# A decoder layer on one Trainium2 core: the output projection as seven products, its weights prepared in the first up projection

## The chip, the cores and the metric

The kernel runs on one core of one Trainium2 chip. The metric is the time of one execution on the device, in microseconds (us); the time before is the median of three executions. One more execution was recorded by the profiler, and every duration quoted below is from it.

PE is the matrix engine (PEld its weight loads), DVE the vector engine, ACT the scalar engine, POOL the general one, SP the engine that issues nearly all DMAs here. Engines run their own instructions in order and wait for each other through semaphores.

## What is computed

One decoder layer on 1024 tokens of width 1024, all in float32:

```python
x = x + 0.5 * swiglu(rmsnorm(x, g1), w_gu1, w_down1)          # first SwiGLU, inner width 2816
z = rmsnorm(x, g_mix) @ w_in                                  # inputs of three branches and their gates
merged = sum(sigmoid(gate_i) * (y_i @ w_branch_i) for i in "abc")
x = x + merged @ w_out                                        # output projection, 1024 x 1024
x = x + 0.5 * swiglu(rmsnorm(x, g2), w_gu2, w_down2)          # second SwiGLU
```

Branch a is a spatial gating unit, b a latent attention over the tokens, c an attention over 256 memory tokens.

## The kernel before, in words

**Layout.** Activations are held with features on the 128 partitions and tokens along the free dimension, in two halves of 512 tokens. `norm.x(half, c)` is feature tile c (of 8) of one half; a tile of 128 x 2 x 512 holds two of them.

**One product.** A float32 value is split into a high part (ACT copy into a rounded type, L139 or L146) and a low part (DVE subtraction, L142 or L147). `mm3` (L158 to L160) multiplies two split operands by three matmuls, high by high, high by low, low by high, of 128 x 128 weights with 128 x 512 tokens.

**Seven products.** The up projections of both SwiGLUs, the gates and the down projections use a scheme of the Strassen-Winograd kind: weights are four blocks A11, A12, A22, A21 (output tile by half of the input features), the activations four blocks b11, b12, b22, b21 (half of the input features by token half), and seven products of sums of blocks take the place of eight. `sum_steps` forms the weight sums s1 to s4 on DVE (L1443), `weights_later` splits them, `unit_steps` runs a unit: 7 products of 4 x 3 matmuls, giving two output tiles for both token halves. A unit's weight pairs are "a" (A11, A12), "s" (s2, s1), "t" (s3, s4) and "l" (A22); each pair takes one buffer of the tag `whi` and one of `wlo`, 5 of each. `up` runs 18 such units (4 to 21) in the first SwiGLU, with PE's order as written and the other engines' orders set by the planner, which lays the program out on a modelled timeline, in program order among what is ready.

**Jobs in the first up projection.** `weight_jobs` splits weights that are needed later (memory attention, latent attention, spatial gating) and writes high and low parts to DRAM. A job (`rounded`) has two steps: issue the load; then split and issue two stores. `up` runs the steps that are due in a unit through `self.extra`, behind the split of "t". There are 14 jobs, and each unit holds about one first and one second step.

**The stage of the change.** Behind the attention, `branch_pairs` multiplies branch b by its weights, gates it (DVE), adds the sum of the other branches (POOL, L574) and splits the result into `merged`. `project` then runs for each token half and output tile c: load w_out's tiles and split them, 8 x 3 matmuls into one PSUM bank, add to x (DVE, L1155), square for the norm (ACT, L1302; summed on DVE, L1307), store every second tile to x2d. Eight output tiles of two halves are 384 matmuls. While half 1 runs, `norm.first()` gives the norm of half 0 four tasks, one behind each of the first four tiles: column sums and root, the scale turned into rows (`norm_scale`, L425), and `part(0)`, `part(1)`, which multiply by gain and scale (L1344), subtract (L1367) and split b22 and t3.

**The second SwiGLU's start.** `units` takes units 0 and 1 together, with the orders of PE, DVE and ACT as written. It begins with s3 t3 and s4 b22 of both units, which need half 0 alone; after `count`=2 and the next of these 16 groups of three matmuls stands the column sum of half 1 (L394), after `turn`=5 its scale (L425), and then half 1's own norm, b11, b21, t2, t1, t4 follow, each made on DVE and ACT just ahead of the product that takes it.

Of the kernel before, what the change touches and what calls it, by code (L numbers as in the profile page):

```python
# [16 lines left out]
P = 128  # L17
# [32 lines left out]
class Kernel:  # L50
# [350 lines left out]
    def turned_sums(self, acc, parts=1, late=False):  # L401


        nc, n = self.nc, acc.shape[-1] // P
        out = self.stat("ts", NT * 2)[:, :n * parts]
        for t0 in range(0, n, 4):
            m = min(4, n - t0)
            b = self.bank()
# [307 lines left out]
    def weight_jobs(self):  # L716

        self.wkv = self.dram.tile([2, 4, 2, P, D], F32, name="wkv")
        jobs = [self.rounded(self.a["mem_w_kv"][g][:, 2 * c:2 * c + 2], self.wkv[g, c])
                for g in range(2) for c in range(4)]  # L720
        self.wqs = self.dram.tile([3, 2, P, H * QK], F32, name="wqs")
        self.wks = self.dram.tile([2, 2, P, D], F32, name="wks")
        self.wss = self.dram.tile([2, P, D], F32, name="wss")

        def causal(x):
            x = x.rearrange("p (g t) -> p g t", g=SGG)
            self.nc.gpsimd.affine_select(
                out=x, in_=x, compare_op=ALU.is_ge, fill=0.0, base=0,
                pattern=[[0, SGG], [1, P]], channel_multiplier=-1,
            )  # L730
# [4 lines left out]
        when = {}  # L735
        for first, some in ((0, jobs), (1, small)):
            for n, job in enumerate(some):
                for f in range(2):
                    at = when.setdefault(first + 2 * n + f, [])
                    at.insert(0 if f else len(at), lambda job=job: next(job))  # L740
        return when
# [358 lines left out]
    def mixer(self, lat):  # L1100
# [36 lines left out]
        merged = [self.hrows() for _ in range(2)]  # L1137
        for _ in self.branch_pairs(
                1, yb, mc, None, each, lambda d, f, x: self.split(*merged[f][d], x)):
            pass  # L1140
        return merged

    def project(self, merged, norm, sink):

        nc, a = self.nc, self.a
        tasks = []
        for half in range(2):
            for c in range(DT):
                w = self.load(a["w_out"][c])
                b = self.bank()  # L1150
                for k in range(DT):
                    self.mm3(b, w[k], merged[half][k], k == 0, k == DT - 1)
                x, parts = norm.x(half, c), 2 if (half, c) == (1, DT - 1) else 1
                for n in self.parts(parts):
                    nc.vector.tensor_tensor(x[:, n], x[:, n], b[:, n], op=ALU.add)  # L1155
                norm.feed(half, c, parts)
                sink(half, c)
                if tasks:
                    tasks.pop(0)()
            tasks = norm.first() if half == 0 else tasks  # L1160
        for t in tasks:
            t()

    def store(self, rows, half, c):

        cols = slice(half * 512, half * 512 + 512)
        n = 1 if half == 1 and c >= DT - 2 else 2
        if n == 1 or c % 2:
            self.nc.sync.dma_start(
                self.out[c - n + 1:c + 1, :, cols].rearrange("c p t -> p c t"),  # L1170
                rows.t[half, c // 2][:, c % 2 - n + 1:c % 2 + 1])


    def run(self):
# [66 lines left out]
        with self.banks("mixps") as self.pm:  # L1241
            merged = self.mixer(latents)
        with tc.tile_pool(name="f2", bufs=1) as fp, self.banks("f2ps") as self.pm:
            rows = Rows(self)
            for half in range(2):
                for p in range(DT // 2):
                    nc.sync.dma_start(rows.take(half, p), x1d[half, p])
            norm = OpNorm(self, rows, lambda: self.g_ffn2)
            ffn = SwiGLU(self, a["ffn2_w_gu"], a["ffn2_w_down"], fp, norm, 2)
            for f in range(2):  # L1250
                ffn.fetch(f, [ffn.w4] * 4)
            self.project(merged, norm, lambda half, c: keep(x2d, norm.t, half, c))
            E = mybir.EngineType
            with tc.manual_schedule(engines={E.PE, E.DVE, E.Activation}):
                ffn.units(
                    (0, 1), (), ([(0, "a")], [(1, "a")]),
                    [lambda: None, lambda: ffn.fetch(2, [self.x4] * 2)],
                    turn=5, third=(2, None, [lambda: ffn.spill(0, ffn.w4, nc.vector)]), count=2)
# [22 lines left out]
class OpNorm:  # L1281
# [7 lines left out]
    def __init__(self, k, rows, gain, scaled=False):  # L1289
        self.k, self.x, self.t, self.gain, self.scaled = k, rows, rows, gain, scaled  # L1290
        self.acc, self.r, self.s, self.op, self.rows = {}, {}, {}, {}, {}
        self.more = []
# [24 lines left out]
    def tokens(self, half):  # L1317
        k = self.k
        more, self.more = self.more, []
        if half == 0 and not self.scaled:  # L1320
            self.s[half] = k.turned_sums(self.acc.pop(half), late=True)
# [10 lines left out]
    def turn(self, half):  # L1332
        k = self.k
        self.s[half] = k.norm_scale(self.r[half], late=k.last is not None)
# [30 lines left out]
    def low(self, p):  # L1365
        b12 = self.norm(0, p)
        self.k.nc.vector.tensor_tensor(b12, self.rows[p][0], b12, op=ALU.subtract)  # L1367
# [11 lines left out]
    def t2(self, p):  # L1379

        t = self.t.t[1, p]
        self.k.nc.vector.tensor_tensor(t, self.t.t[0, p], t, op=ALU.add)
        return t

    def t1(self, p):

        t = self.t.t[0, 2 + p]
        self.k.nc.vector.tensor_tensor(t, t, self.t.t[1, p], op=ALU.subtract)
        return t

    def t4(self, p):

        t = self.t.t[1, 2 + p]
        self.k.nc.vector.tensor_tensor(t, t, self.t.t[1, p], op=ALU.subtract)
# [3 lines left out]
class Seven:  # L1398
# [11 lines left out]
    def __init__(self, k, w, pool, norm):  # L1410
        self.k, self.nc, self.norm, self.w, self.pool = k, k.nc, norm, w, pool
        self.quad, self.made, self.mark, self.extra = {}, {}, None, []
# [20 lines left out]
    def sum_steps(self, f, rooms=None, order="3241"):  # L1433
# [5 lines left out]
        of = {"3": (s3, a11, a21, ALU.subtract), "2": (s2, a22, s3, ALU.subtract),  # L1439
              "4": (s4, a12, s2, ALU.subtract), "1": (s1, a21, a22, ALU.add)}  # L1440
# [13 lines left out]
    def weights_later(self, f, part, room=None):  # L1454
        k, q = self.k, self.quad[f]
# [21 lines left out]
    def unit_steps(self, f, after=False):  # L1477
# [32 lines left out]
        w |= self.weights(f, "l")  # L1510
        del self.quad[f]
# [134 lines left out]
class Gates(Seven):  # L1646
# [49 lines left out]
    def run(self):  # L1696
# [10 lines left out]
        with k.tc.manual_schedule(engines={E.PE}):  # L1707
            for n, f in enumerate(units):
# [4 lines left out]
                self.extra += self.later[:1] + [lambda x=x: got.append(next(x)) for x in jobs.get(n, ())]  # L1713
# [173 lines left out]
class SwiGLU(Seven):  # L1887
# [22 lines left out]
    def emit(self, f, i, half, row, ps, into=None):  # L1910
# [10 lines left out]
        elif half == 0:  # L1921
            self.add(h, row, ps)
        else:
            self.add(row, row, ps)
            self.gate(f, 0, row)
# [150 lines left out]
    def up(self, first, jobs={}):  # L2076

        with self.k.tc.manual_schedule(engines={mybir.EngineType.PE}):
            for f in range(first, FT):
                if f not in self.quad:  # L2080
                    self.fetch(f)
                self.extra += jobs.get(f - first, [])
# [178 lines left out]
def layout(inputs):  # L2261
# [47 lines left out]
    r["w_out"] = cols(i["w_out"].reshape(D, D), P)  # L2309
# [22 lines left out]
```

## Time and profile before

| | |
|---|---|
| median of 3 executions | 2163.2 us (2163.03 to 2163.79) |
| the profiled execution | 2163.03 us, span from first to last instruction 2161.3 us |
| granted PE clock, mean | 0.999 of full speed |
| DMA | 342.56 MB, mean 158 GB/s, nearly all through SP's queue |
| first up projection | 98.2 to 440.9 us |
| attention's end, last branch, output projection | about 1384 to 1527 us |
| first two units of the second SwiGLU | from 1527 us |

A row of a timeline reads: start, duration, engine, line, operation, output<-input by the program's names, shape, count, and in brackets the idle time ahead of it with what ended it. A row of a window reads: from and to, length, then busy time with instructions of PE, PEld, DVE, ACT and POOL, the granted clock, the busy share of the 16 DMA engines and the GB/s they moved. A row of the DMA view gives size and the median time from issue to landing. A "busy" PE is not PE at its peak, because overlapping matmuls have modelled ends; starts are recorded.

### The profile page before, as it was taken

The page shows a single profiled execution, that of the slowest core. Times are in us where ns is not written, and L with a number is a line of the kernel's source. Part 1 is how long each engine was busy: PE and PEld are TensorE (multiplying, and loading weights), DVE is VectorE, ACT ScalarE, POOL GpSimd, SP SyncE. Part 2 cuts the span into 40 slices and gives each one's busy share as a digit, 9 for nine tenths or more (in the row PEclk, how much of TensorE's full clock was granted, in tenths as well). Part 3 has the DMA queues.
Part 4 walks back from the last instruction along what each step waited for, and adds up shares of the span by engine and source line. Part 5 has one row for each costly group of instructions (what it writes and reads, how often), then busy time and mean ns, then how long its engine had stood idle before and what let it go on. Part 6 is the DMA issues. An engine that isn't in the chain of part 4 may idle for free.

```text
span 2161.3 us, 27448 instructions
## 1 busy us (share of the span) xinstructions
PE 2151.9 (100%) x10112; PEld 1797.8 (83%) x10112; DVE 1572.1 (73%) x2371; ACT 910.3 (42%) x1486; POOL 255.0 (12%) x256
## 2 busy tenths in 40 slices
PE   9999999999999999999999999999999999999999
PEld 6888888888887888888988889988888888888887
DVE  7966666679889657655786679886876666657884
ACT  6433333243455434433555378833433223224332
POOL 0011111100000000000123311240011212110000
PEclk9999999999999999999999999999999999999999
DMA  4264555385332445641587832293133332347443
GB/s 148 92 220 159 190 180 175 119 318 193 118 124 94 147 164 180 223 149 61 212 283 259 314 105 69 75 348 104 40 127 103 110 97 100 103 144 288 169 129 104
DMA packets 137175, 342.56 MB, mean 158 GB/s; under 512 B 21713, under 2 KB 30033, under 8 KB 137041
## 3 DMA queue, kind: packets, MB, share of 16 engines
q1 hardware_dynamic: 136896, 340.81, 45.9%
q8 instruction: 79, 1.29, 0.2%
q14 instruction: 56, 0.45, 0.1%
q10 hardware_dynamic: 144, 0.00, 0.0%
HBM read 230.90 MB, written 109.86 MB: 158 GB/s over the span
## 4 chain that ended last, share of the span: by engine, by line
PE 91%; DVE 6%; ACT 1%; DMA 1%; issue 1%; SPq 0%; POOL 0%; ACTq 0%; DVEq 0%; POOLq 0%
PE one L158 15%; PE one L159 15%; PE one L160 15%; PE bank L158 13%; PE bank L159 13%; PE bank L160 13%; PE mm L158 1%; PE mm L159 1%; PE mm L160 1%; PE bank L1019 1%; PE one L1967 1%; DVE w L147 1%; DVE wlo L147 1%; DVE pr L997 1%; DVE wlo L142 1%
## 5 line engine op out<-in xcount | busy, mean ns | idle before, releaser
L146 ACT CAST whi<-x 128x1024 fp32r<-128x1024 f32 x202 | 192.3, 955 | 414.4 <-DVE x L1443 170.4
L147 DVE TENSOR_TENSOR wlo<-x,whi 128x1024 fp32r<-128x1024 f32 x202 | 241.2, 1195 | 58.9 <-ACT whi L146 19.6
L1471 DVE TENSOR_TENSOR t<-t,one 128x512 f32<-128x512 f32 x188 | 128.9, 686 | 190.8 <-PE one L160 190.7
L158 PE MATMUL bank<-h,whi 128*128 128x512 f32 x636 | 247.9, 390 | 0.0
L160 PE MATMUL bank<-h,wlo 128*128 128x512 f32 x636 | 247.5, 389 | 0.0
L159 PE MATMUL bank<-h,whi 128*128 128x512 f32 x636 | 247.5, 389 | 0.0
L158 PE MATMUL one<-h,whi 128*128 128x512 f32 x508 | 199.0, 392 | 0.0
L159 PE MATMUL one<-h,whi 128*128 128x512 f32 x508 | 198.4, 390 | 0.0
L160 PE MATMUL one<-h,wlo 128*128 128x512 f32 x508 | 198.3, 390 | 0.0
L158 PE MATMUL one<-w,whi 128*128 128x512 f32 x432 | 168.5, 390 | 0.0
L159 PE MATMUL one<-w,whi 128*128 128x512 f32 x432 | 168.1, 389 | 0.0
L160 PE MATMUL one<-w,wlo 128*128 128x512 f32 x432 | 168.1, 389 | 0.0
L142 DVE TENSOR_TENSOR wlo<-w,whi 128x1024 fp32r<-128x1024 f32 (+2 forms) x112 | 114.4, 1036 | 67.3 <-ACT whi L139 67.1
L139 ACT CAST whi<-w 128x1024 fp32r<-128x1024 f32 (+2 forms) x112 | 98.8, 901 | 149.8 <-PE one L159 55.6
L2067 POOL TENSOR_TENSOR raw<-raw 128x512 f32<-128x512 f32 x38 | 57.0, 1499 | 794.8 <-DVE raw L1908 684.8
L160 PEld LDWEIGHTS bank<-h,wlo 128*128 128x128 f32 x636 | 119.4, 188 | 24.9
L159 PEld LDWEIGHTS bank<-h,whi 128*128 128x128 f32 x636 | 119.4, 188 | 24.6
L158 PEld LDWEIGHTS bank<-h,whi 128*128 128x128 f32 x636 | 119.4, 188 | 24.4
L158 PE MATMUL bank<-whi 128*128 128x512 f32 x352 | 136.9, 389 | 0.0
L159 PE MATMUL bank<-wlo,whi 128*128 128x512 f32 x352 | 136.9, 389 | 0.0
L160 PE MATMUL bank<-whi,wlo 128*128 128x512 f32 x352 | 136.9, 389 | 0.0
L160 PEld LDWEIGHTS one<-h,wlo 128*128 128x128 f32 x508 | 95.8, 189 | 20.1
(406 smaller groups left out, 4892.2 us busy)
## 6 DMA issues: line engine op xcount, KB each, us to landing
x<-in_ffn_w_gu_dram SPq DMA_DIRECT2D x78, 512.0 KB, 5.1
w<-tdt SPq DMA_DIRECT2D x40, 512.0 KB, 4.2
gate<-raw SPq DMA_DIRECT2D x33, 512.0 KB, 3.0
tdb<-raw SPq DMA_DIRECT2D x64, 256.0 KB, 2.1
h<-in_ffn_w_down_dram SPq DMA_DIRECT2D x64, 256.0 KB, 6.0
w<-tdb SPq DMA_DIRECT2D x30, 512.0 KB, 5.1
tdt<-w SPq DMA_DIRECT2D x48, 256.0 KB, 2.4
x<-in_w_gate_dram SPq DMA_DIRECT2D x22, 512.0 KB, 5.9
```

The costliest lines, as they stand in the source:

```text
L139: i = self.nc.scalar.copy(hi, src)
L142: return (eng or self.nc.vector).tensor_tensor(lo, src, hi.bitcast(F32), op=ALU.subtract)
L146: self.nc.scalar.copy(hi, src)
L147: return lambda: self.nc.vector.tensor_tensor(lo, src, hi.bitcast(F32), op=ALU.subtract)
L158: i = mmul(out, s[0], m[0], start=first, stop=False, **kw)
L159: mmul(out, s[0], m[1], start=False, stop=False, **kw)
L160: self.last = mmul(out, s[1], m[0], start=False, stop=last, **kw)
L997: nc.vector.tensor_tensor_reduce(out=pr[:, :m], in0=sc[:, :m], in1=self.mask[:, m0:m0 + m], scale=1.0, scalar=-NEG, op0=ALU.add, op1=ALU.m ...
L1019: nc.tensor.transpose(b[:, at:at + P], prs[t][:, kk * P:(kk + 1) * P], self.ident)
L1471: return self.nc.vector.tensor_tensor(out, x, y, op=ALU.add)
L1967: k.last = nc.tensor.matmul(b, w, norm.x(half, c), start=c == 0, stop=c == DT - 1)
L2067: sub = lambda d, x, y: (eng or nc.gpsimd).tensor_tensor(d, x, y, op=ALU.subtract)
```

## The change

The output projection becomes seven products too, four output tiles deep, and runs in a new function `merge` together with branch b. `project` and the call of `branch_pairs` for branch b are gone. w_out is laid out by the host as blocks A11, A12, A22, A21, each in two groups g of 128 x 1024.

```diff
+        for u, b in product("a", self.single, ws, "b11", True):      # product 1, A11 b11, banks kept
+            add(1, 2 * u + 1, b, ALU.subtract)
...
+        for u, b in product("x", self.bank, w2, "t2", True):         # 2
...
+        for u, b in product("x", None, ws, "t1", False):             # 3, on top of 2
...
+        for u, b in product("x", None, w2, "b22", False):            # 4, on top
+            add(0, 2 * u, b)
+            norm.feed(0, 2 * u)
...
+        for u, b in product("y", self.bank, ws, "t3", True):         # 5
+            add(0, 2 * u + 1, b)
+            norm.feed(0, 2 * u + 1)
+            sink(0, 2 * u + 1)
+        ws = weights(6)
+        later()
+        norm.take = self.single
+        for u, b in product("a", None, w2, "b21", False):            # 6, on top of 1
+            add(1, 2 * u, b)
+            if u == 1:
+                with self.tc.high_priority(offset=600):
+                    norm.sums(0)
+            elif u == 3:
+                norm.turn(0)
+                norm.take = None
+                norm.part(0)
+            norm.feed(1, 2 * u)
+        for u, b in product("y", None, ws, "t4", False):             # 7, on top of 5
+            parts = 2 if u == 3 else 1
+            if u == 0:
+                norm.part(1)
+            add(1, 2 * u + 1, b, parts=parts)
+            norm.feed(1, 2 * u + 1, parts)
+            sink(1, 2 * u + 1)
```

(The comments are added here.) `product` runs u = 0 to 3, each 4 blocks x 3 matmuls, into four banks. Ahead of it, `merge` runs branch b in 16 steps ordered by block (b11, b12, b22, b21), with gating and addition both on DVE, and splits b11, t2, b22, t1, t3, b21, t4. `weights(n)` only loads split parts from DRAM, four loads of 512 KB a product. `manual_schedule` keeps the order of PE and SP as written throughout `merge`; the loads of x from DRAM (`load`) stand behind `weights(1)`. The two token halves change places (x1d, x2d and `store` are indexed the other way), and signs in the seven products are turned (`plus`), with the same number of operations.

The weights are made in the first up projection. Their sums are formed in DRAM by DMAs that POOL issues, plain copies and adding ones, one step in each of units 0 to 10 of `up`:

```diff
+        def move(d, x, more):
+            self.nc.gpsimd.dma_start(d, x, max_dma_last_dim=2 * D, **({"accum_op": ALU.add} if more else {}))
...
+        steps = ((s3, A11, False), (s1, A21, False), (s3, A21, True), (s1, A22, True),
+                 (s2, s3, False), (s2, A22, True), (s4, s2, False), (s4, A12, True))
+        return [lambda x=x: blocks(*x) for x in steps] + [first, second, third]
```

The eight `steps` are two DMAs of 512 KB each, for w_out; `first` (4 x 512 KB), `second` (6 x 256 KB) and `third` (4 x 256 KB) form the sums of units 0 and 1 of the second SwiGLU. Then 20 more jobs (`rounded`) split them: 14 for the seven weights of the output projection in two groups, 6 for "a", "t" and "s" of the second SwiGLU's units 0 and 1. Jobs have two places in a unit now: the old one behind "t" (`ahead`), and one behind the split of "l" (`behind`):

```diff
+        made = [self.rounded(x.unsqueeze(1), d) for x, d in parts]
+        early = [j for pair in zip(jobs, small) for j in pair]
+        early += jobs[len(small):] + small[len(jobs):] + made[17:]
+        ahead, behind = ({n: [] for n in range(FT)} for _ in range(2))
+        step = lambda job: lambda: next(job)
+        for n, job in enumerate(made[:17]):
+            behind[n].append(step(job))
+            ahead[n + 1].append(step(job))
+        for n, job in enumerate(early):
+            ahead[n].append(step(job))
+            behind[n].insert(0, step(job))
+        for n, f in enumerate(out):
+            ahead[n].append(f)
+        return ahead, behind
```

So units 0 to 16 each run both steps of one old (or late) job and the first step of a new one, and the second step of the new one runs in the next unit. In the second SwiGLU, `weights_later` loads "a", "t" and "s" of units 0 and 1 split from DRAM (`ffn.pre`) in place of forming sums and splitting; "t" is loaded in `merge` (`later`), "a" and "s" in `units`, and A22 is loaded raw by `low` and split as before.

More of the change, by code (lines that the diff above doesn't have):

```diff
@@ L399, in token_sums, with turned_sums @@
         return b
-    def turned_sums(self, acc, parts=1, late=False):
+    def turned_sums(self, acc, parts=1, late=False, bank=None):
         nc, n = self.nc, acc.shape[-1] // P
@@ L734, in weight_jobs @@
         small += [self.rounded(self.a["sg_w"], self.wss, causal)]
[L735 to L741, printed above, removed]
+        out = self.wide_sums()
+        parts = self.wide_parts()
+        made = [self.rounded(x.unsqueeze(1), d) for x, d in parts]
[12 more added lines that the diff above has]
+        return ahead, behind
     def row_jobs(self):
@@ L1136, in mixer @@
         yb = self.attention(self.branch_pairs(2, yc, md, self.x4, first + each[8:], sink_c))
[L1137 to L1162, printed above, removed]
+        return yb, mc
@@ new lines, in wide_parts @@
+    def wide_parts(self):
+        self.wo = self.dram.tile([7, 2, 2, P, D], F32, name="wo")
+        self.f2 = self.dram.tile([2, 3, 2, P, D], F32, name="f2w")
+        A11, A12, A22 = range(3)
+        s3, s1, s2, s4 = self.wosum
+        at = lambda x, g: self.a["w_out"][g, x] if isinstance(x, int) else x[g]
+        out = [(at(x, g), self.wo[n, g]) for n, x in ((0, A11), (5, A12), (6, A22), (4, s3), (2, s1), (1, s2), (3, s4))
+               for g in range(2)]
+        for f in range(2):
+            src = self.a["ffn2_w_gu"][f][:, :2], *self.f2sum[f]
+            out += [(x.rearrange("p a w -> p (a w)"), self.f2[f, n]) for n, x in enumerate(src)]
+        return out
@@ L1281, with __init__ @@
 class OpNorm:
[L1289 removed]
+    def __init__(self, k, rows, gain, scaled=False, plus=False):
         self.k, self.x, self.t, self.gain, self.scaled = k, rows, rows, gain, scaled
         self.acc, self.r, self.s, self.op, self.rows = {}, {}, {}, {}, {}
[L1292 removed]
+        self.more, self.take, self.plus = [], None, plus
     def feed(self, half, c, parts=1):
@@ L1320, in tokens @@
         if half == 0 and not self.scaled:
-            self.s[half] = k.turned_sums(self.acc.pop(half), late=True)
+            self.s[half] = k.turned_sums(self.acc.pop(half), late=True, bank=self.take)
         else:
@@ L1333, in turn @@
         k = self.k
-        self.s[half] = k.norm_scale(self.r[half], late=k.last is not None)
+        self.s[half] = k.norm_scale(self.r[half], late=k.last is not None, bank=self.take)
     def norm(self, half, p):
@@ L1920, in emit @@
             return lambda: self.gate(f, 1, c)
-        elif half == 0:
-            self.add(h, row, ps)
-        else:
-            self.add(row, row, ps)
-            self.gate(f, 0, row)
+        else:
+            out = h if half == 0 else row
+            x, y, op = (ps, row, ALU.subtract) if self.plus else (row, ps, ALU.add)
+            self.nc.vector.tensor_tensor(out, x, y, op=op)
+            if half:
+                self.gate(f, 0, row)
     def start(self, load_x, load_g):
@@ L2081, in up @@
                     self.fetch(f)
-                self.extra += jobs.get(f - first, [])
+                for todo, job in zip((self.extra, self.behind), jobs):
+                    todo += job.get(f - first, [])
                 self.unit(f)
```

197 lines of the change are left out of this document (172 added, 25 removed).

## The prediction

> **What bounds the kernel now.** I read the page first (busy time, slices, chain), then the windows of the two stages that the change touches, then DVE's and PE's timeline at the boundary between them.
>
> ```profile
> span 2161.3 us, 27448 instructions
> PE 2151.9 (100%) x10112; PEld 1797.8 (83%) x10112; DVE 1572.1 (73%) x2371; ACT 910.3 (42%) x1486; POOL 255.0 (12%) x256
> ...
> PE 91%; DVE 6%; ACT 1%; DMA 1%; issue 1%; SPq 0%; POOL 0%; ACTq 0%; DVEq 0%; POOLq 0%
> ```
>
> PE is busy all the time and 91% of the chain that ended last. "Busy" alone proves little, as ends are modelled; the windows (span, then PE, PEld, DVE, ACT, POOL, clock, DMA share, GB/s) prove more:
>
> ```profile
> 98.20:440.90 342.70, 342.70 (x1513) 283.75 (x1512) 230.07 (x294) 111.06 (x141) 47.74 (x34) 1.00 0.53 181
> 98.20:307.60 209.40, 209.40 (x925) 173.37 (x924) 143.84 (x187) 70.30 (x88) 27.68 (x20) 1.00 0.56 190
> 421.88:440.92 19.04, 19.04 (x86) 15.77 (x85) 8.13 (x12) 4.41 (x7) 1.29 (x1) 1.00 0.88 312
> 1395.20:1527.20 132.00, 132.00 (x589) 109.33 (x588) 95.69 (x137) 47.81 (x78) 26.40 (x17) 1.00 0.58 215
> 1445.00:1450.00 5.00, 5.00 (x24) 4.14 (x23) 1.97 (x4) 1.99 (x4) 0.00 (x0) 1.00 1.03 419
> 1527.20:1563.50 36.30, 36.12 (x166) 29.55 (x165) 34.31 (x48) 18.50 (x22) 0.00 (x0) 1.00 0.08 29
> ```
>
> The first row is the up projection of the first SwiGLU: 18 units of 7 products of 12 matmuls, 1512 in 342.7 us, so 226.7 ns each at clock 1.00, one unit in 19.04 us, no gap between them. The fourth is the last branch and the output projection, equally dense. So a matmul taken out is worth 226.7 ns, if nobody keeps PE waiting. The last row shows where somebody nearly does: behind the output projection DVE works 34.31 of 36.30 us.
>
> **The change, part by part.**
>
> *Matmuls.* The output projection's own rows, between 1395.2 and 1527.2 us:
>
> ```profile
> L160 PE MATMUL bank<-h,wlo 128*128 128x512 f32 x128 | 49.8, 389 | 0.0
> L158 PE MATMUL bank<-h,whi 128*128 128x512 f32 x128 | 49.8, 390 | 0.0
> L159 PE MATMUL bank<-h,whi 128*128 128x512 f32 x128 | 49.8, 389 | 0.0
> ```
>
> 384 before; seven products of 4 outputs x 4 blocks x 3 are 336. The 192 of the branch and the transposes of the norm stay. 48 x 0.2267 = **-10.9 us**, all on the path.
>
> *The norm of the first token half moves late.* Its DVE rows before, then PE's turn of its scale and the end of the projection:
>
> ```profile
> 1493.93 0.69 DVE L1155 TENSOR_TENSOR x<-x,bank 128x512 f32<-128x512 f32 x1 [1.78 <-PE bank L160]
> 1494.54 5.35 DVE L1344 SCALAR_TENSOR_TENSOR x<-x,c_ffn_norm,bank 128x512 f32<-128x512 f32 x8
> ...
> 1501.61 1.22 DVE L147 TENSOR_TENSOR h<-x,h 128x1024 fp32r<-128x1024 f32 x1
> 1502.74 1.22 DVE L1367 TENSOR_TENSOR x<-x,x 128x1024 f32<-128x1024 f32 x1
> 1503.88 0.68 DVE L1155 TENSOR_TENSOR x<-x,bank 128x512 f32<-128x512 f32 x1
> ...
> 1527.05 0.75 DVE L1155 TENSOR_TENSOR x<-x,bank 128x256 f32<-128x256 f32 x2 [3.31 <-PE bank L160]
> 1528.02 0.76 DVE L1307 TENSOR_TENSOR t<-t 128x256 f32<-128x256 f32 x2 [0.21 <-ACT t L1302]
> ```
>
> ```profile
> 1493.73 0.60 PE L425 MATMUL bank<-ident,rs_y 128*128 128x128 f32 x4
> ...
> 1526.62 0.39 PE L160 MATMUL bank<-h,wlo 128*128 128x512 f32 x1
> 1526.85 0.39 PE L158 MATMUL one<-h,whi 128*128 128x512 f32 x1
> ...
> 1528.89 0.95 PE L394 MATMUL bank<-ones,t 128*128 128x1 f32 x8
> ```
>
> Before, the scale was turned at 1493.73, 33 us ahead of the projection's end at 1526.85, and half 1's products hid the norm. In the new `merge` half 0's scale is turned only behind product 6, so the two `part` calls share DVE with the whole of product 7, 10.9 us of PE. Set T=0 at the end of product 6. PE turns the scale (0.4 us), runs product 7 to T=11.2, then three groups of s3 t3 to T=13.3, and stands before the column sums of half 1 (L394, behind the third group as before). DVE, at start-to-start times (0.60 for 512 columns, 1.13 for 1024), must by then have done: add and feed of product 6's last output, 1.2; eight norm steps, 5.35; two subtractions, 2.3; four low parts, 4.5; add and feed of outputs 0 to 2, 3.6; the last output in two parts with its square, 1.75 (1527.05 to 1528.78). Sum 18.7 from T=0.3, so T=19.0, and PE waits 19.2 - 13.3 = 6 us, first at t3's second pair, then at L394. That is the naive order. If b22's two low parts come after the column sums, it is 3.5 us. ACT's copies can open gaps and make it 7. I take **+5.5**, near the naive order, since b22 is put ahead of t3 in the code. Nothing else of DVE's is late by then: in products 1 to 6 I count 4 to 10 us of it per 10.9.
>
> *Behind the sums.* Weights a, t and s of the first two units come split from DRAM: DVE loses eight sums and six low parts, 8 x 0.6 + 6 x 1.13 = 11.6 us, ACT six copies. Only three low parts lie in the tight stretch:
>
> ```profile
> L147 DVE TENSOR_TENSOR wlo<-w,whi 128x1024 fp32r<-128x1024 f32 x3 | 3.6, 1217 | 0.0
> ...
> 1560.44 0.69 DVE L1471 TENSOR_TENSOR raw<-t,one 128x512 f32<-128x512 f32 x1
> ...
> 1561.28 0.47 PE L158 MATMUL one<-x,whi 128*128 128x512 f32 x1 [0.18 <-DVE raw L1471]
> ```
>
> 3.4 us less for DVE there, but PE had only a gap of about 0.5 us to lose: **-0.5**. The rest ran under PE anyway: nothing. So did the 32 copies and subtractions of w_out's parts; the 16 additions that come from POOL to DVE (16 x 0.6) fill that space.
>
> *Loads in the merge.* 28 x 0.52 = 14.7 MB of split weights replace 8.4 MB of w_out (2.1 MB for the second SwiGLU stay 2.1): 215 GB/s over 132 us is 28.4 MB, now 34.7 MB in 121 us, 287 GB/s, under the 312 that left PE full in the third window. SP's order is written out, so a blocked issue holds all behind it: product 7's weights stand behind the store of half 0's last rows, which waits for DVE until about T=-9.5 (product 5's end at -10.9, an add and a square); four loads that land 8.5 us behind their issue, the slowest row below, are there by T=0, used at T=0.4. Cost 0; if that cover fails, 1 to 3.
>
> *Twenty more weight jobs in the first up projection.* Each is a load, a copy on ACT (about 1), a subtraction on DVE (1.13) and two stores: 20 x 1.13 = 23 us more in 342.7, DVE from 230 to 253 (74%), ACT from 111 to 132. What the weights of a unit have to spare, DVE rows and their first use on PE:
>
> ```profile
> 237.22 0.69 DVE L147 TENSOR_TENSOR wlo<-x,whi 128x512 fp32r<-128x512 f32 x1 [3.38 <-DMA wkv<-wlo]
> ...
> 240.96 1.22 DVE L147 TENSOR_TENSOR wlo<-x,whi 128x1024 fp32r<-128x1024 f32 x1
> ...
> 247.80 0.39 PE L158 MATMUL one<-x,whi 128*128 128x512 f32 x1
> ...
> 250.52 0.39 PE L158 MATMUL bank<-h,whi 128*128 128x512 f32 x1
> ```
>
> A11's low part ends 8.3 us early, A22's 9.9. But six pairs a unit now go through five buffers, and the first row already waits for a job's store. Five buffers are 95 us per unit. The shortest holdings: a and s 11 each, t 8, l 5, and a job 11 (rows below: 3.9 load, 2.2, 4.9 store), twice: 57. It fits: **0**, at most some 0.5 us a unit if landings pass 10 us.
>
> ```profile
> wlo<-in_mem_w_kv_dram SPq DMA_DIRECT2D x8, 512.0 KB, 3.9
> wkv<-wlo SPq DMA_DIRECT2D x8, 512.0 KB, 4.9
> ```
>
> *Sums in DRAM.* 30 DMAs from POOL in units 0 to 10, 13.1 MB. The trace shows no DMA issued by POOL, and none that adds. POOL is busy 27.68 of 209.4 us there; even 3 us an issue is 90. Queued behind them are the spill's subtractions, and behind those the hidden rows' buffers. A gain is excluded, as nothing else gets shorter. On the engines: 190 GB/s, plus a job a unit (1.57 MB, 83), plus 63, is 335 GB/s. The rows of 312 (share 0.88) and 419 (1.03) put the full rate between 355 and 407, so the share is 0.82 to 0.94. I take **0**.
>
> **Sum.** 2161.3 - 10.9 + 5.5 - 0.5 = 2155.4 span; with 0.9 for the small risks above (product 7's loads, the five buffers) 2156.3. The profiled execution took 2163.03, 1.7 outside its span, 0.2 under the median of 2163.2. So 2158.0, and **2158.2** against that median: 5.0 us or 0.23% faster. What a measurement can tell from no change is about 0.2%, 4.3 us: the forecast lies just beyond it.
>
> **The rivals.**
>
> *The backlog is hidden.* If the planner has DVE do t3 first and the sums of half 1 between, with b22 behind, the wait shrinks to 1 to 3 us: 2161.3 - 10.9 + 2 - 0.5 + 1.9 = 2153.8. Against it: the sum of 18.7 us in 13 hardly bends.
>
> *The boundary eats the gain.* Weights a of the first two units are loaded behind the stores of half 1's rows on SP, from about T=19.3; used at 28.5. Loads of 512 KB from DRAM in a loaded spell land in 4.9 to 8.5 us.
>
> ```profile
> whi<-wkv SPq DMA_DIRECT2D x5, 512.0 KB, 8.5
> ```
>
> With four issues of 0.33, 19.3 + 1.3 + 8.5 = 29.1: up to 1 us; with DVE's backlog at 7 and 1 to 3 for product 7's weights late, the boundary costs 9 to 11: 2162 to 2164, no change.
>
> *The DMA engines become the bound in units 0 to 10 (slower).* Every byte of the DRAM sums is read and written there, and 6.8 MB of the additions also read their target. If the engines pay for each of these moves, the demand is 190 + 83 + 125 + 33 = 431 GB/s against 407: 209.4 x (431/407 - 1) = 12 us, so 2158.2 + 12 = 2170. It decides from where demand passes the full rate, then fetches of the next unit's weights land late and PE waits in each unit. For it: 335 is near 355 already. Against: the sums may lag four units before anybody reads them, and at share 0.88 PE lost nothing. [...]
>
> **How the numbers follow.** Forecast 0.51, of which 0.37 beyond 4.3 us and 0.14 short of it; backlog hidden 0.14; boundary eats the gain 0.17; DMA bound 0.18. Faster 0.51, same 0.31, slower 0.18. The range goes from the hidden backlog's 2153 to 2168, inside the DMA case, and leaves out about 0.17.
>
> **What would show it.** Right: 10,064 matmuls; product starts in the merge 10.9 us apart with no idle; then one wait of 4 to 7 us on PE at L394's place, released by DVE, with DVE full from product 6's end; the up projection still 342.7 us with DVE near 74% and DMA share 0.8 to 0.95 in units 0 to 10. Wrong: PE idle inside the up units, released by DMA or by ACT's copies (the third rival or the five buffers); PE waiting in the merge on loads; or no wait at L394.

## The result, and the profile after

| | median | all executions | ratio to before, 95% interval |
|---|---|---|---|
| before | 2163.11 us | 2162.89 to 2163.79, 4 | |
| after | 2191.68 us | 2187.72 to 2193.64, 4 | 1.0129 [1.0112, 1.0147] |

The change makes the kernel 28.6 us slower; the forecast was 5 us faster, and its range ended at 2168. The profiled execution of after took 2187.72 us. The head of its page:

```profile
span 2186.0 us, 27492 instructions
PE 2154.0 (99%) x10064; PEld 1791.0 (82%) x10064; DVE 1588.1 (73%) x2387; ACT 909.7 (42%) x1466; POOL 255.3 (12%) x270
```

The 48 matmuls are gone (10,112 to 10,064), the span is 24.7 us longer, and PE still reads 99%. So the busy share shows nothing. I took instead the recorded starts of all matmuls and subtracted, from each step between two starts, what such a matmul takes in a dense stretch (0.2267 us for 512 columns). What is left is time that PE lost:

| PE's lost time, us | before | after |
|---|---|---|
| start, 0 to 98 | 18.7 | 23.2 |
| first up projection, to 460 | 0.0 | 12.3 |
| gates, down projections, attention, to 1390 | 9.7 | 9.0 |
| last branch begins, 1390 to 1470 | 0.6 | 10.4 |
| seven products, second SwiGLU begins, to 1640 | 0.9 | 8.6 |

With PE's first instruction 1.8 us later, that is +1.8 + 4.5 + 12.3 - 0.7 + 9.8 + 7.7 - 10.9 = 24.5 of the 24.7. This profiled execution is the fastest of after's four; the 3.9 us by which the medians lie further apart are in no row here. There are four places, and two of them are not in the prediction at all. Each has its rows.

**The start.** POOL's timeline, then PE's first wait in the view of waits (engine, tile and line, releaser: us in total, times, longest):

```profile
1.38 1.40 POOL L1159 DMA_DIRECT2D wosum<-in_w_out_dram  x2 [0.33 <-issue]
2.86 0.34 POOL masks.py:199 TENSOR_SCALAR_AFFINE_SELECT ident<-ident 128x128 f32<-128x128 f32 x1
...
107.79 0.91 POOL L1159 DMA_DIRECT2D wosum<-in_w_out_dram  x1 [9.29 <-issue]
129.24 1.29 POOL L2276 TENSOR_TENSOR raw<-raw 128x512 f32<-128x512 f32 x1 [20.53 <-DVE raw L2116]
```

```profile
PE bank L231 <- POOL ident masks.py:199: 3.2, 1, 3.2
```

The DRAM sums are written in units 0 to 10, but nothing that they need comes from a unit. So the planner put them ahead of everything: the first stands before the identity matrix that PE's first transposes take, the last before the first spill. They run beside the first loads of x. In each experiment below that issues them later, PE's first instruction is back at 1.5 us, as before.

**The up projection.** Windows (before's whole up projection was dense: 1513 matmuls in 342.7 us):

```profile
98.00:455.00 357.00, 349.29 (x1523) 284.19 (x1522) 254.60 (x322) 132.25 (x165) 48.61 (x36) 1.00 0.76 264
```

PE's and ACT's waits there, and one such place in the timeline:

```profile
PE bank L158 <- ACT t L1696: 6.3, 12, 1.7
```

```profile
ACT whi L139 <- DMA wlo<-in_mem_w_kv_dram: 27.3, 7, 5.1
...
ACT whi L139 <- DMA wlo<-wosum: 14.3, 3, 5.0
```

```profile
300.69 0.33 SPq L699 DMA_DIRECT2D wlo<-in_mem_w_kv_dram  x1
...
306.21 1.04 ACT L139 CAST whi<-wlo 128x1024 fp32r<-128x1024 f32 x1 [5.12 <-DMA wlo<-in_mem_w_kv_dram]
307.16 0.58 ACT L1696 COPY t<-bank 128x512 f32<-128x512 f32 x1
...
307.79 0.50 PE L158 MATMUL bank<-h,whi 128*128 128x512 f32 x1 [1.70 <-ACT t L1696]
```

Read it from below. PE's third product writes into the bank that ACT's copy of the first product (L1696) has still to read. The copy stands behind a cast, and the cast waits for a job's load that SP issued 5.5 us before. PE waits for a weight whose split parts are first loaded again at 1073 us.

**The last branch begins.** SP, its wait, then PE:

```profile
1383.29 0.46 SPq L1229 DMA_DIRECT2D t<-gate  x1
1418.74 0.36 SPq L1231 DMA_DIRECT2D w<-mc  x1
1419.20 0.41 SPq L1229 DMA_DIRECT2D t<-gate  x1
1419.67 0.42 SPq L100 DMA_DIRECT2D raw<-in_w_branch_dram  x1
```

```profile
SPq L1231 <- DVE x L142: 34.9, 1, 34.9
```

```profile
1419.68 0.39 PE L160 MATMUL bank<-x,wlo 128*128 128x512 f32 x1
1426.09 0.80 PE L158 MATMUL bank<-x,whi 128*128 128x512 f32 x1 [6.02 <-ACT whi L139]
1426.68 0.63 PE L159 MATMUL bank<-x,whi 128*128 128x512 f32 x1
1427.11 0.63 PE L160 MATMUL bank<-x,wlo 128*128 128x512 f32 x1
```

SP's order is as written in `merge`. Its first load of mc goes into a tile of the new pool, whose space the attention gives up only at about 1418.7. SP issues nothing for 35 us, and the branch weights of tiles 2 and 3, needed at 1419.9, stand behind it. Behind the wait ten matmuls step at 0.43 us in place of 0.227.

**The second SwiGLU begins.** DVE, then PE:

```profile
1532.51 0.69 DVE L1266 TENSOR_TENSOR x<-x,one 128x512 f32<-128x512 f32 x1 [0.59 <-PE one L160]
1533.12 5.35 DVE L1539 SCALAR_TENSOR_TENSOR x<-x,c_ffn_norm,one 128x512 f32<-128x512 f32 x8
...
1547.19 2.35 DVE L147 TENSOR_TENSOR h<-x,h 128x1024 fp32r<-128x1024 f32 x2
1549.46 1.55 DVE L1502 TENSOR_TENSOR t<-t 128x512 f32<-128x512 f32 x3
```

```profile
1543.67 0.39 PE L158 MATMUL one<-h,whi 128*128 128x512 f32 x1
1546.06 0.50 PE L159 MATMUL one<-h,whi 128*128 128x512 f32 x1 [2.00 <-DVE h L147]
...
1549.59 0.79 PE L159 MATMUL one<-h,whi 128*128 128x512 f32 x1 [1.31 <-DVE h L147]
1550.19 0.63 PE L160 MATMUL one<-h,wlo 128*128 128x512 f32 x1
```

This is the forecast backlog: DVE is full from 1532.5, the last output of product 6, to 1551.0. Two waits, 3.9 us by steps, and 4.7 more behind them, nearly all in matmuls and column sums at the slow step.

### The profile page after: what moved, and what is told of

The parts are those of the page before. It is cut to its first block, busy times and chain, and to the rows that moved or that the text cites. A ratio compares the mean times of both kernels' runs of the same rounds, so it can differ in the third digit from the quotient of the medians.

```text
span 2186.0 us, 27492 instructions
## 1 busy us (share of the span) xinstructions
PE 2154.0 (99%) x10064; PEld 1791.0 (82%) x10064; DVE 1588.1 (73%) x2387; ACT 909.7 (42%) x1466; POOL 255.3 (12%) x270
## 3 DMA queue, kind: packets, MB, share of 16 engines
q0 software_dynamic: 5344, 13.11, 2.8%
## 4 chain that ended last, share of the span: by engine, by line
PE 85%; DVE 6%; DMA 6%; ACT 2%; issue 1%; SPq 0%; POOL 0%; ACTq 0%; DVEq 0%; POOLq 0%
PE one L158 15%; PE one L159 15%; PE one L160 15%; PE bank L158 12%; PE bank L159 11%; PE bank L160 11%; DMA x<-in_x_dram 1%; PE mm L158 1%; PE mm L159 1%; PE mm L160 1%; DMA wlo<-in_mem_w_kv_dram 1%; DVE wlo L142 1%; PE bank L1028 1%; DVE pr L1006 1%; DVE wlo L147 1%
## 5 line engine op out<-in xcount | busy, mean ns | idle before, releaser
L158 PE MATMUL bank<-h,whi 128*128 128x512 f32 x588 | 230.9, 393 | 6.3 <-ACT t L1696 6.3
L160 PE MATMUL bank<-h,wlo 128*128 128x512 f32 x588 | 229.0, 389 | 0.0
L159 PE MATMUL bank<-h,whi 128*128 128x512 f32 x588 | 228.9, 389 | 0.0
L1677 DVE TENSOR_TENSOR t<-t,one 128x512 f32<-128x512 f32 x149 | 102.2, 686 | 169.5 <-PE one L160 169.4
L159 PE MATMUL one<-h,whi 128*128 128x512 f32 x540 | 211.5, 392 | 3.3 <-DVE h L147 3.3
L158 PE MATMUL one<-h,whi 128*128 128x512 f32 x540 | 212.0, 393 | 0.0
L160 PE MATMUL one<-h,wlo 128*128 128x512 f32 x540 | 211.3, 391 | 0.0
L158 PEld LDWEIGHTS bank<-h,whi 128*128 128x128 f32 x588 | 110.4, 188 | 34.3 <-ACT t L1696 11.9
L160 PEld LDWEIGHTS bank<-h,wlo 128*128 128x128 f32 x588 | 110.4, 188 | 23.2
L159 PEld LDWEIGHTS bank<-h,whi 128*128 128x128 f32 x588 | 110.4, 188 | 22.3
L159 PEld LDWEIGHTS one<-h,whi 128*128 128x128 f32 x540 | 101.9, 189 | 25.5 <-DVE h L147 4.4
```

What stands on the lines that cost most here:

```text
L158: i = mmul(out, s[0], m[0], start=first, stop=False, **kw)
L159: mmul(out, s[0], m[1], start=False, stop=False, **kw)
L160: self.last = mmul(out, s[1], m[0], start=False, stop=last, **kw)
L1677: return self.nc.vector.tensor_tensor(out, x, y, op=ALU.add)
```

## The experiments

Theory A: each of the four losses is an order, something urgent queued behind something that is not, on ACT, SP, POOL or DVE. Rival B: the DMA engines are short of throughput in the up projection, and orders only choose who waits. Rival C: five wide buffers are too few for six pairs a unit. B and C make other forecasts for edits that change the order and no byte.

All results, with PE's lost time by stage in the order of the table above:

| run | median us | ratio, 95% | start | up | middle | branch | boundary |
|---|---|---|---|---|---|---|---|
| after | 2191.7 | 1.0129 [1.0112, 1.0147] | 23.2 | 12.3 | 9.0 | 10.4 | 8.6 |
| e1 sums held | 2200.9 | 1.0177 [1.0163, 1.0191] | 17.1 | 38.9 | 9.3 | 10.8 | 8.5 |
| e2 cast after copy | 2188.4 | 1.0123 [1.0109, 1.0137] | 25.8 | 8.0 | 10.4 | 10.3 | 8.3 |
| e3 branch first | 2181.8 | 1.0086 [1.0072, 1.0099] | 25.1 | 12.0 | 9.3 | 1.9 | 7.2 |
| e4 b22 on POOL | 2190.5 | 1.0126 [1.0112, 1.0139] | 24.6 | 14.0 | 9.0 | 10.0 | 5.3 |
| e5 sums at 36 | 2194.4 | 1.0144 [1.0130, 1.0158] | 20.8 | 23.5 | 9.4 | 10.8 | 8.3 |
| e6 held + cast | 2192.7 | 1.0129 [1.0113, 1.0144] | 17.4 | 25.1 | 9.0 | 11.7 | 8.5 |
| e7 jobs spaced | 2178.5 | 1.0070 [1.0057, 1.0082] | 23.0 | 0.6 | 12.0 | 9.6 | 5.6 |
| e8 t3 first | 2185.4 | 1.0099 [1.0085, 1.0113] | 25.4 | 12.9 | 8.2 | 10.6 | 4.5 |
| e9 = e7 + e3 + e8 | 2167.6 | 1.0026 [1.0016, 1.0036] | 28.7 | 0.4 | 11.4 | 1.5 | 4.6 |
| e10 = e9, sums at 17 | 2162.8 | 1.0000 [0.9991, 1.0009] | 17.9 | 5.1 | 10.8 | 1.4 | 4.5 |
| e11 = e9, sums held | 2176.5 | 1.0062 [1.0049, 1.0074] | 17.5 | 14.7 | 12.0 | 1.8 | 4.5 |
| e12 = e9, sums at 36 | 2167.4 | 1.0024 [1.0015, 1.0034] | 21.2 | 5.8 | 10.6 | 1.5 | 4.6 |
| e13 = e9, sums shared out | 2157.9 | 0.9980 [0.9971, 0.9988] | 17.5 | 0.7 | 11.3 | 1.2 | 4.6 |
| e14 = e13, t3 sooner | 2157.9 | 0.9977 [0.9968, 0.9985] | 18.7 | 0.4 | 11.8 | 0.8 | 3.5 |
| e15 = e11, an eighth | 2156.6 | 0.9972 [0.9960, 0.9983] | 18.8 | 2.1 | 9.6 | 0.7 | 4.5 |

The stages come from one profiled execution of each, the median from all; the two differ by up to 6.3 us (e1). The start varies most: in the seven runs that leave the sums at the start (after, e2, e3, e4, e7, e8, e9) it loses 23.0 to 28.7. e15 is no kernel to use, as it leaves out seven eighths of every addition. In the code excerpts below the comments are added, and `run(x)` stands for calling what is in the list x and emptying it.

**e1: the sums held to their units.**

```diff
+            k.gate = nc.gpsimd.tensor_copy(k.stat("gate", 1), v1[:, :1])   # in units 0 to 10, ahead of the unit's jobs
...
-            self.nc.gpsimd.dma_start(d, x, ...)
+            self.after(self.nc.gpsimd.dma_start(d, x, ...), self.gate)
```

> The changed kernel with its DRAM sums held back: in units 0 to 10 of the up projection POOL reads one column of a row that the unit has just made and issues that unit's sums behind it, so none is issued before about 105 us, and one step goes out per unit. Everything else as in the changed kernel (2191.7 us). Theory A (each loss is a wait behind a neighbour in an in-order engine or queue; here the sums' traffic delays the first loads of x): the stretch from 0 to 98 us gets back 5 to 7 us and PE's starts there are as in the kernel before; the up projection keeps its 12 us of waits, since these come from ACT's order: 2184 to 2188. Rival B (the DMA engines' throughput is the bound in the up projection): the sums, 63 GB/s more in units 0 to 10 on top of some 255, bring the waits there from about 0.7 us a unit to 2 or more, and the whole is no better than the changed kernel: 2190 to 2200.

The start came back as A had it (17.1), but the up projection lost 38.9, not 12: A's figure for the whole fell; B's (2190 to 2200) was reached, and passed by 0.9. The waits keep their name, and longer ones take its place:

```profile
PE bank L158 <- ACT t L1696: 18.8, 8, 5.5
PE one L158 <- DVE t L1677: 6.5, 6, 2.3
```

So bytes do matter there; whether as such, or by way of a load that an in-order engine waits for, this run cannot say.

**e2: the early job's cast behind the copy.**

```diff
-        nc.scalar.copy(p1, a)
+        k.hold = nc.scalar.copy(p1, a)     # a cast made while hold is set is ordered behind it
+        run(self.held)                     # the early job's second step, of the unit before
+        k.hold = None
```

> The changed kernel with one difference: the second step of each early job (cast, subtraction, two stores) stands behind the next unit's copy of its first product on ACT, not ahead of it. Loads, stores, bytes and buffers are the same, each early job holds its buffer some 5 us longer. Theory A: PE's wait for that copy (releaser ACT, line 1696) goes away in nearly all units, the up projection takes 343 to 346 us in place of 355: 2178 to 2183. Rival B (DMA throughput): waits stay as long and only change the name of their releaser, 2188 to 2193. Rival C (five wide buffers are too few): holding one longer makes the waits longer, over 2193.

The wait for the copy (L1696) is gone from the view, and between 98 and 250 us PE lost 0.1. But 8.0 stayed, later on, under another name. DVE's waits say whose:

```profile
DVE wlo L147 <- DMA wo<-wlo: 40.0, 14, 4.2
```

The unit's own low part waits for a buffer that a job's store still reads. That is rival C, brought out by holding each early job some 5 us longer. Theory A was a part of the cause (12.3 to 8.0), and the median lies where B had it (2188 to 2193); e7 answers B.

**e3: the branch weights first.**

```diff
+        for dt in (0, 2): y = self.load(self.a["w_branch"][1, dt // 2]); w[dt], w[dt + 1] = y[:4], y[4:]
         for n in range(4): ahead(n)
```

> The changed kernel with both first loads of the branch weights (feature tiles 0 to 3) ahead of the first load of mc in SP's written order. Theory A: the load of mc waits for room that the attention gives up, and the branch weights behind it come late only for that; now they are there early, PE's wait of 6 us at 1426 goes, and so do the matmuls at half rate behind it: minus 8 to 10, 2182 to 2184. Rival D (mc itself is what the branch needs): mc lands as late as before, the four banks of the branch fill up and PE waits for DVE's gating a few us later: minus 0 to 4, 2188 to 2192.

A by its numbers: 10.4 to 1.9, and 9.9 us off the median. mc still goes out at 1420.64, as late as before; nobody but the branch weights had suffered from that, so rival D falls.

**e4: POOL makes b22's low parts.**

```diff
-        return k.split_later(hi, lo, src)
+        return (lambda: k.split(hi, lo, src, k.nc.gpsimd)) if self.plus and name == "b22" else k.split_later(hi, lo, src)
```

> The changed kernel with the two low parts of b22 (128x1024 each, 1.13 us each on DVE) made by POOL, which is idle there. Theory A (the wait at the start of the second SwiGLU is DVE's backlog): PE's wait for t3's first pair falls from 2.2 to about 1, for the second from 1.7 to about 0.6, and if a shorter wait no longer halves the rate of the matmuls behind it, another 4 us go: 2185 to 2189, at least 2.3 less than the changed kernel. Rival E (the end is set elsewhere, by the chain from the last output's square to half 1's scale): the waits move to the column sums or the scale, 2191 to 2193. POOL's copies may take so long that b22 itself is late; then PE waits for POOL and nothing is won.

The first wait went and the stage lost 5.3 in place of 8.6, but only 1.2 us came off the median, within the spread of both and between the ranges of A and E. DVE did not get back what it gave away:

```profile
1546.16 2.36 POOL L142 TENSOR_TENSOR h<-x,h 128x1024 fp32r<-128x1024 f32 x1 [5.34 <-ACT h L139]
...
1546.33 3.27 DVE L147 TENSOR_TENSOR h<-x,h 128x1024 fp32r<-128x1024 f32 x1
```

A subtraction that takes 1.22 us alone took 3.27 beside POOL's, and it made the low part for which PE stood 2.9 us. The run says nothing against the backlog, but it is no way to relieve it.

**e5: all sums behind a row of 36 us.** The same `after`, on a POOL read of a row that ACT copies at the end of the start's products.

> The changed kernel with all its DRAM sums behind one POOL read of a row that ACT makes at about 36 us, when the first loads of x are done and before the up projection; nothing else is held. So the start is free of them, and most of their bytes go out between 36 and 110 us, where the kernel before used a third of the DMA engines. Theory A (the sums hurt at the start because they stand ahead of the first transposes' matrix on POOL and beside the loads of x, and hurt in the up projection, as the run with the sums held there showed, because they delay loads that an in-order engine waits for): the start gets back 5 to 6.5 us and the up projection loses as much as in the changed kernel, 12 us, or 1 to 3 more: 2185 to 2189. Rival B (bytes are bytes: the DMA engines are short over the whole first 450 us): what is won at the start is lost in the first units, 2190 to 2194.

Start 2.4 better, up projection 11.2 worse: what B said, a little past its range. With the orders as they were, the first units paid for all.

**e6: e1 and e2 together.**

> Both edits of the first two experiments of the up projection at once: sums held to units 0 to 10, and the early job's cast behind the next unit's copy on ACT. It tells apart why the sums in the units cost 26 us more waits there than the changed kernel has. Theory A' (longer landings, but paid only through ACT's order): with the order mended most of the 39 us of waits go, up projection under 355 us, 2178 to 2188. Rival B (throughput): the loads of the unit's own weights and the jobs' stores land late whatever ACT's order is, waits stay over 25 us in the up projection, 2195 or more. Rival C (five buffers): in between, with PE's waits led by DVE's low parts that wait for a job's store, 2188 to 2195.

The median fell into C's range, the waits (25.1) to where B had them; this did not settle what the rest was. e7, e11 and e15 did.

**e7: both jobs moved to where their loads have landed.**

```diff
-            ahead[n + 1].append(step(job))           # made: behind the split of t
+            held[n + 1].append(step(job))            # behind the next unit's copy of its first product
...
-            behind[n].insert(0, step(job))           # early: behind the split of l
+            tail[n].append(step(job))                # at the unit's end, not before its sixth product
```

> The changed kernel with both jobs of a unit moved: the job loaded behind the split of l is cast right behind the next unit's copy of its first product (held some 5 us shorter), the early job's cast stands at the unit's end and not before its sixth product. Bytes and buffers are the same. Theory A with C (ACT's order first, then five buffers of which each job holds one too long): waits in the up projection fall from 12 to 2 to 6 us, 2180 to 2186, below the run that moved the early cast alone (2188.4). Rival B (throughput): no better than that run, 2188 to 2192.

12.3 fell to 0.6, better than A with C had it. The window, with every byte of after in it:

```profile
98.00:455.00 357.00, 356.67 (x1574) 294.99 (x1573) 261.20 (x332) 134.08 (x172) 52.30 (x38) 1.00 0.78 273
```

1574 matmuls where after had 1523, at a higher DMA share, 0.78 against 0.76. B cannot be why after's up projection is slow: the engines moved more while PE waited for nothing.

**e8: t3 of both units first.** PE's 16 groups sorted, `count` 7, `turn` 11, and b22's low parts on DVE behind the last sum of squares.

> The changed kernel with another order at the start of the second SwiGLU and the same work: PE runs the eight groups of t3 of both units first and b22's eight behind, the column sums of half 1 stand behind the eighth group and the scale behind the twelfth, and DVE makes b22's two low parts behind the last sum of squares. Theory A (DVE's backlog of the norm meets PE too early): the two waits of 2.2 and 1.7 us shrink to under 1.5 together, the matmuls at half rate behind them (4 us) go, b11 waits 1 to 2: 2184 to 2188. Rival E (the chain from the last output to half 1's scale sets the end anyway): the wait moves to b11, 2190 to 2193.

8.6 to 4.5, and 6.3 us off the median, of which other stages can hold a part. The waits are three of about 0.9, and behind them no run of slow steps:

```profile
PE one L159 <- DVE h L147: 2.4, 3, 0.9
```

**e9: the three mended orders.**

> The changed kernel with the three mended orders together: both jobs of a unit spaced, the branch weights ahead of mc on SP, t3 first at the start of the second SwiGLU. Same DMAs, same matmuls, DRAM sums still at the start. If the three losses are independent, as theory A has it, the sum is 2191.7 - 11.7 (up projection 12.3 to 0.6) - 8.5 (merge 10.4 to 1.9) - 4.1 (second SwiGLU 8.6 to 4.5) = 2167.4, range 2164 to 2171; what is left against the sum without waits is then the start (6) and the boundary (4). If they are not (one wait hides behind another), 2172 or more.

2167.6 against 2167.4 worked out, and the three stages lose what they lost when mended alone (0.4, 1.5 and 4.6 against 0.6, 1.9 and 4.5): these three losses are independent.

**e10, e11, e12: e9 with the sums in other places.** e10 holds them behind POOL's read of the last tile of x, e11 as e1, e12 as e5.

> The kernel of the three mended orders, and the DRAM sums behind one POOL read of the last tile of x as it lands (about 17 us): the identity matrix on POOL and the loads of x go first. Theory A: the start gets back 3 to 6 us, and with the jobs spaced the up projection bears the sums' later end: 2161 to 2165. Rival B (throughput of the first units): what the start wins the first units lose, as in the run with the sums at 36 us: 2166 to 2172.

> The kernel of the three mended orders, with the sums held to units 0 to 10, one step a unit, as the code was read in the prediction. It settles whether the DMA engines bear the sums there once ACT's order and the five buffers no longer stand in the way. Theory A (order alone): up projection under 347 us, start as in the kernel before, 2160 to 2165. Rival B (throughput, the prediction's third rival: share of the DMA engines near its full rate): 10 to 20 us of waits in units 0 to 10, 2171 to 2182.

> The kernel of the three mended orders, with the sums behind ACT's row of about 36 us. In the changed kernel this cost 11 us more waits in the first two units, of which 6 in one place where DVE stood behind a job's store and beside POOL's own issues. Theory A: with the jobs spaced this goes, the start is as in the kernel before: 2161 to 2165. Rival B: the first units stay 8 to 11 us longer: 2168 to 2174.

e10 fits A, e11 fits B, e12 lies between them, nearer B: what the start won the first units lost. In e11 the three orders are mended and PE still loses 14.7. Its window over most of units 0 to 10, and then e9's, where the sums have gone before:

```profile
98.00:300.00 202.00, 197.16 (x862) 161.04 (x861) 149.51 (x182) 72.03 (x91) 50.32 (x54) 1.00 0.95 309
```

```profile
98.00:300.00 202.00, 201.96 (x891) 166.76 (x890) 152.07 (x194) 75.45 (x96) 24.34 (x18) 1.00 0.75 262
```

What the sums take is read from the DMA queues (packets, MB, share of the 16 engines' span): in e11 SP's queue, then POOL's, which carries the sums alone, and then POOL's in e15, the next run.

```profile
q1 hardware_dynamic: 149152, 383.28, 50.3%
q0 software_dynamic: 5344, 13.11, 2.8%
```

```profile
q0 software_dynamic: 4320, 7.15, 1.2%
```

2.8% of 2171.4 us are 61 us of all 16 engines for 13.11 MB, 216 GB/s, where SP's queue makes 351. The difference between the two windows, 0.20 x 202 = 40 us, is less because a part of the sums lies behind the window and e11 does less of its other work in it.

PE lost 6.8 of the 14.7 in this window and nearly all the rest before 330 us, but only 1.4 before 250, with the engines 0.94 to 0.96 busy from the start. So the high share alone did not make PE wait. The longest waits still come by way of ACT's order:

```profile
PE one L158 <- ACT whi L146: 5.4, 3, 3.5
```

**e15: e11 with an eighth of each addition.**

```diff
+            d, x = (d[..., :d.shape[-1] // 8], x[..., :x.shape[-1] // 8]) if more else (d, x)
```

> The kernel with the three mended orders and the sums held to units 0 to 10 (2176.5, 14.7 us of waits in the up projection), where every adding DMA is cut to an eighth of its columns: the same 30 issues in the same places on POOL, the orders of all other engines the same, 6.3 + 0.9 MB in place of 13.1. Seven eighths of the additions are left out. Theory F (bytes, counted twice, on top of a busy stretch): waits fall to 3 to 7 us, 2164 to 2170. Rival G (the issues): waits stay at 12 or more, 2174 to 2177.

The same 30 issues, and 14.7 fell to 2.1, below F's range, as the median did: the bytes cost, not the issues. The 5.96 MB left out took about 35 of the 61 us, per byte twice the time of SP's queue (some 170 GB/s against 351), so F's "counted twice" holds for the additions. e1's 38.9 us come apart: 24.2 were orders and buffers (to e11's 14.7), 12.6 the bytes of the additions on a stretch already busy. How much of the 12.6 is throughput as such, and how much a later load that ACT's queue still waits for, these runs do not tell apart.

**e13, e14: the sums shared out.** Those of w_out at 17 us, those of the second SwiGLU two a unit in units 2 to 8. e14 also puts product 7's adds behind t3's low parts.

> The kernel of the three mended orders, with the sums shared out: those of w_out (16 DMAs) behind the last tile of x at about 17 us, those of the second SwiGLU (14 DMAs) two a unit in units 2 to 8, each pair behind a POOL read of that unit's row. Theory F (the sums cost twice their bytes on the DMA engines, and PE waits only where they stand on top of a stretch already over 0.8 busy): the early stretch ends some 35 us sooner, the wait of 3.6 us at 120 goes, units 2 to 8 stay under 0.9 busy and lose at most 1 us: 2157 to 2160, under the kernel before (2162.5). [...]

> The same, and product 7's first adds stand behind t3's low parts on DVE, so that both t3 pairs are ready before the second SwiGLU starts. The two waits of 1.0 and 0.9 us there go; the column sums come no sooner, and b11's wait (1.1) may grow by as much. Theory A: 1 to 2 us under the run of the shared-out sums, 2155.5 to 2158.5. Rival E (the chain to half 1's scale sets the end of that stretch): the same as that run within 0.5.

```profile
98.00:300.00 202.00, 202.00 (x891) 166.94 (x890) 153.18 (x191) 74.87 (x95) 42.68 (x41) 1.00 0.86 293
```

This is e13: 0.86 busy, no wait. It beats the kernel before by 0.20% [0.12, 0.29]. In e14 two of the boundary's waits went and 1.1 us of lost time, but the median is the same, as rival E had it; with executions from 2155.7 to 2159.8 a gain of 1 us cannot be told from none, so that the chain to half 1's scale sets the end is not shown. Both are 5 us under before, with the matmuls and the DMAs' bytes of the change that was 28.6 over.

## Why the prediction was wrong, step by step

- *Matmuls, -10.9.* Right: 10,064, and from 1450 until the wait at 1543.7 the products run without a gap.
- *The norm moves late, +5.5.* The mechanism was right: 18.7 us of DVE from the turn of the scale was forecast, and DVE is full for 18.5, from 1532.5 to 1551.0, with the operations that were counted. The place was nearly right (t3's first pair and second, with nothing left for the column sums). The size was off: 7.7 us. The waits were 3.9, less than the 6 of the working, but they drew 4.7 of slow matmuls and column sums behind them, and those the sum did not have.
- *Behind the sums, -0.5.* No row shows it apart; it lies inside the 7.7.
- *Loads in the merge, 0.* The products' loads were on time, so the working on product 7 was right. But "SP's order is written out, so a blocked issue holds all behind it" was asked of product 7 alone, not of the first issue of `merge`. Missed: +9.8, undone by two loads put ahead (e3).
- *Twenty more weight jobs, 0.* The step that failed is "It fits". I counted DVE's spare time and each buffer's hours, and e7 bears both out: the same jobs in the same five buffers, with 0.6 us lost. (There one job holds its buffer some 5 us shorter; in e2, with one held 5 us longer, DVE waited 40 us for stores, so the buffers had less to spare than 57 of 95.) What I did not ask is what stands behind each new waiting instruction on its own engine. The early job's cast had some 5 us for a load, and PE's next copy behind it. Cost: +12.3.
- *Sums in DRAM, 0.* "In units 0 to 10" failed first: I took the place in the text for the place in time, with nothing that ties a DMA on POOL to its unit. They cost +6.3 at the start. Had they stayed in the units, the third rival's price, 12 us, would have been near: e11 loses 14.7 at share 0.95, e13 nothing at 0.86. That is near by number and not by working. The rival has demand beyond the full rate from unit 0 on; e11 lost next to nothing for the first 150 us. And its bytes are too dear: 125 + 33 GB/s over 209 us are 33 MB, 81 to 93 us of the engines at the prediction's 355 to 407 GB/s, where the queue's row has 61. e11's window moved 309 GB/s at share 0.95; what sets the sums' rate, no run here shows.

None of the three rivals came true: the backlog was not hidden, the boundary ate 7.7 and not the whole gain, and the DMA engines did not bind in after. The term of the matmuls held, and the mechanism of the norm; most of the loss, 28 of 35 us (the 24.5 and the 10.9 saved), came from orders that I had not read, ACT's, SP's and POOL's. With these mended, e13 gives 2157.9, where the sum had 2158.2. That they meet is in part luck: e13 also has t3 first, so the norm costs 3.7 and not 5.5, its start is 1.2 better than before's, and the middle, which the sum left alone, is 1.6 worse; why, no run shows.

## What to carry to other kernels

For every step that is added, ask of each of its instructions which engine's queue it stands in, what it waits for there, and what urgent work is queued behind it; buffer and busy-time sums come after that. Where a planner sets the order, ask what ties a piece of work to its place in the code: the sums here had no data dependence on their units and went out at 1.4 us, not at 98. Here 11 us of saved matmuls were lost three times over in queues.

## What the runs showed of the hardware

- *The long waits cost more than their length.* Behind all 17 waits on PE of 3.1 to 6.9 us in after and e1 to e12 (the first 60 us left out) the matmuls step at 0.43 us, from 0.6 us after the wait on, 6 to 13 times: 1.2 to 2.6 us more. The granted clock shows it too: in after it was 0.50 from 1424.1 us, inside the wait of 6.0 us, to 1430.9, and 1.00 on either side; over 1405 to 1450 that makes 0.92. At the boundary it was 0.50 from 1546.9 to 1557.2. Shorter waits went both ways: behind the four lone waits of 2.2 to 2.4 us in the up projection no matmul is slow, behind two lone ones of 2.0 us (e8 at 307 us, e1 at 365) eight are, and behind the boundary's pair of 2.2 and 1 to 2 us 4 to 13. What decides which of the shorter waits are followed by slow matmuls, these runs do not show.
- *A DVE subtraction took longer beside POOL's.* It took 3.27 us in e4's rows, against 1.22 without POOL, and ended 1.1 us after POOL's did. e4's eight norm steps (SCALAR_TENSOR_TENSOR) took 5.35 us beside POOL's subtraction of 2.40, and 5.35 in after without it.
- *DRAM sums by DMA* took the 16 engines 61 us for 13.1 MB in e11, 216 GB/s, less than the 351 of SP's queue in the same run and the 419 of the prediction's row. The additions were the dear part: 5.96 MB of them took about 35 us (e11's row less e15's), some 170 GB/s.
